# Projections of three gates made ahead and kept in DRAM, in a two-layer trunk kernel

## The chip, the cores and the metric

The kernel runs on one core of one Trainium2 chip. The metric is device time in microseconds: 1871.26 us, median of three runs (1866.83 to 1872.24). The profile below is of one further execution, 1869.99 us.

## The reference

Two layers over 2048 positions of width 1024. Layer 0 mixes with a gated short convolution, layer 1 with gated causal window means. Each mixer is followed by a gate that adds a projection of a 256 wide embedding `p` of the position. This projection, `p[i] @ ple_w_proj[i]`, depends on the inputs only.

```python
h = x
for i in range(DEPTH):                       # DEPTH = 2
    hn = rmsnorm(h, norm_mix[i])
    if i % 2 == 0:
        h = h + short_conv_mixer(hn, a_w_in, a_w_conv, a_w_out)
    else:
        h = h + pool_mixer(hn, b_w_in, b_w_grp, b_scale, b_w_out)
    gate = jax.nn.sigmoid(rmsnorm(h, ple_norm[i]) @ ple_w_gate[i])
    h = h + gate * (p[i] @ ple_w_proj[i])
return rmsnorm(h, final_norm)
```

## The kernel before

Positions lie in four chunks (`ch` 0 to 3) of 512 columns, features in eight tiles of 128 partitions. All products run in a split form: an operand is cast to a high part (ScalarE) and its remainder is taken (VectorE), and `mm` adds three matmuls, high by high (L202), high by low (L203), low by high (L204). So each weight and each activation tile costs one cast on ScalarE and one subtraction on VectorE (L106 and L107 for a loaded block of 128x1024, called a granule; L230, L231 and L236, L237 for an activation tile).

Granules come in the order of a list `order`, with a look-ahead `look` of three (one in the head). The pools are small: 4 raw blocks, 4 split weights, 28 split activations (`act`), 10 tiles `h`, 10 work tiles `wk`, 7 banks of PSUM (`mm`). Granules of kind "w" split into the weight ring, those of kind "p" (embedding) and "pt" (projection and group weights) into `act` tiles. All loads and stores are issued by SyncE's queue, in order.

The stages: a head; then twice (super-chunk `sc`) `mixer_a` for two chunks together, with products in pairs (`pair_steps`) whose 28 operands x11, x21, t2, t1, t3, x22, t4 (four tiles each) are sums of normalised x tiles; then for each of the two chunks `mixer_out` (L573), `gate(0)` (L604), `mixer_b`, `mixer_out` and `gate(1)`.

A gate makes for each of eight tiles `k` 24 matmuls of the dense product and 6 of the projection (`gate_mm`, L584), and `gate_out` (L597) multiplies by the root of the mean square `rb`, takes the sigmoid, multiplies by the projection (L601) and adds to `h` (L602). Until `rb` is there tiles are held in PSUM. The mean square comes from `Stat`: squares on ScalarE, additions on GpSimd (L260), then `fin1` and `fin2`, two small matmuls with ones and a few VectorE steps. `finals` multiplies the finished chunk by its scale, eight operations on VectorE at once (L627), and stores it; `hooks` call such pieces between the products of the next stage.

In the head x of chunks 0 and 1 is loaded, its squares are added by sixteen fp32 matmuls with ones (L717), then normalised (L473), subtracted and added (L476) and split (L231). Beside it `fold` multiplies the group weights of the pooling mixer into its input weights, 48 matmuls of 256 columns for each of four folds, kept in DRAM (`wcomb`). Folds 0 and 1 stand in the head, 2 and 3 (`late_folds`, L735) inside the first pairs.

The operands of the second super-chunk are prepared earlier: `prepare(kk)` (four normalisations L473, four sums L476) writes them to `n_dram`, called at tile 2 of `gate(1)` of chunk 0, of `mixer_out` A, of `gate(0)` and of `mixer_out` B of chunk 1. In `gate(1)` of chunk 1, the turn, `X.ahead` loads and splits two of them per tile, 14 of 28.

The order of instructions on each engine is set when the kernel is built, by a scheduler; on the chip each engine takes its own in that order.

Of the kernel before, what the change touches and what calls it, by code (L numbers as in the profile page):

```python
# [9 lines left out]
F32 = mybir.dt.float32  # L10
# [5 lines left out]
P = 128  # L16
# [30 lines left out]
def trunk_kernel(ctx: ExitStack, tc: tile.TileContext, xT, xN, pT, wts, par, out):  # L47
# [112 lines left out]
    def gate_order(layer, ch):  # L160
        base = W_GATE[layer]
        r = [("p", layer * NCH + ch)]
        for h in range(2):
            r += [("pt", base + 8 + h)] + [("w", base + 4 * h + o) for o in range(4)]
        return r

    for ch in range(NCH):
        if ch % 2 == 0:
            order += [("sum", (0, 0)), ("sum", (1, 0))]
            order += [("pt", W_GRP + 1), ("w", W_UT + 4), ("w", W_UT + 5)] if ch == 0 else []  # L170
            order += [("sum", (0, 1))]
            order += [("w", W_UT + 6), ("w", W_UT + 7)] if ch == 0 else []
            order += [("sum", (0, 2)), ("sum", (0, 3))]
# [37 lines left out]
    def psum():  # L211
        return pm.tile([P, T], F32, tag="mm", name="mm")
# [187 lines left out]

    def mixer_a(sc, X, between):
        ys = []
        for j in range(KT):
            cv_steps, zb_steps = pair_steps(2 * j, X), pair_steps(2 * j + 1, X)
            if j == 0:
                next(cv_steps)
                next(zb_steps)
                between(0)
                next(cv_steps)
                between(1)  # L410
            cs1, cs2, v1, v2 = pair_of(cv_steps)
# [172 lines left out]
    def gate_mm(w, wp, pt, a, k, c0, c1):  # L584
# [19 lines left out]
    def gate(layer, ch, a, hs, s_in, next_gain, extra):  # L604
        hooks.extend([s_in.fin1, s_in.fin2])
        s = Stat()
        nxt = []
        pt = next_granule(("p", layer * NCH + ch))
        base = W_GATE[layer]
        held = []  # L610
        for k in range(KT):
            if k % 4 == 0:
                wp = next_granule(("pt", base + 8 + k // 4))
            held.append((k,) + gate_mm(next_granule(("w", base + k)), wp, pt, a, k, 0, T))
            if s_in.rb is None:
# [106 lines left out]
    load_chunk(0)  # L722
    square_sums(0)
    wg = load_granule(("pt", W_GRP))
    us = [load_granule(("w", W_UT + i)) for i in range(2)]
    fold(0, wg, us)
    load_chunk(1)
    square_sums(1)
    X = Operands(first_operand(x, stats))
    X("x11")  # L730
    us = [load_granule(("w", W_UT + 2 + i)) for i in range(2)]
    fold(1, wg, us)
    wg2 = []

    def late_folds(i):  # L735
        if i == 0:
            wg2.append(next_granule(("pt", W_GRP + 1)))
        fold(2 + i, wg2[0], [next_granule(("w", W_UT + 4 + 2 * i + c)) for c in range(2)])
        if i == 1:
            look[0] = LOOK  # L740

# [102 lines left out]
```

## Time and profile before

| | before |
|---|---|
| median of 3 runs | 1871.26 us (1866.83 to 1872.24) |
| profiled execution | 1869.99 us, span 1868.2 us |
| TensorE (PE) busy | 1819.3 us, 97% |
| VectorE (DVE) busy | 1298.1 us, 69% |
| ScalarE (ACT) busy | 746.4 us, 40% |
| GpSimd (POOL) busy | 261.6 us, 14% |
| mean granted TensorE clock | 0.990 |

Busy shares are means over stages. A window of the trace is read by the count of TensorE's instructions in it, since a waiting or slow TensorE shows as fewer of them. A timeline row gives the start, the length, the line, and in brackets the idle time before the instruction and what ended it.

### The profile page before, as it was taken

How to read it: one execution, taken by the hardware profiler on the slowest of the kernel's cores; microseconds unless marked ns; L12 is line 12 of the kernel's file. 1: busy time of each engine (PE TensorE's matmuls, PEld its weight loads, DVE VectorE, ACT ScalarE, POOL GpSimd, SP SyncE). 2: the span in 40 equal slices, each digit the busy share in tenths (PEclk: the TensorE clock that was granted, in tenths of full speed). 3: DMA queues.
4: the chain of work that ended last, by engine and by line, in shares of the span. 5: the costliest groups of instructions: out<-in, count | busy, mean ns of one | idle time of the engine just before them, and what ended most of it. 6: DMA issues, size and time to landing. Idle time of an engine off the chain costs nothing.

```text
span 1868.2 us, 21507 instructions
## 1 busy us (share of the span) xinstructions
PE 1819.3 (97%) x8217; PEld 1499.2 (80%) x8217; DVE 1298.1 (69%) x1777; ACT 746.4 (40%) x1076; POOL 261.6 (14%) x233
## 2 busy tenths in 40 slices
PE   8799999999999998999998999999999999999997
PEld 5688888888888886888876888888888888888897
DVE  5966766676686766787677665766658666768665
ACT  6533333354345434433443333334433344443332
POOL 1000000021212121211110000001121122120010
PEclk9899999999999999999999999999999999999999
DMA  7311111262343455334534111115323242622221
GB/s 271 113 62 62 68 62 62 85 197 87 109 154 125 176 191 182 121 101 150 170 115 141 53 60 63 65 65 175 124 79 102 91 147 102 203 79 96 97 91 46
DMA packets 70647, 212.21 MB, mean 114 GB/s; under 512 B 7824, under 2 KB 9872, under 8 KB 70544
## 3 DMA queue, kind: packets, MB, share of 16 engines
q1 hardware_dynamic: 70544, 210.84, 33.1%
q8 instruction: 64, 1.05, 0.2%
q14 instruction: 39, 0.32, 0.1%
HBM read 186.69 MB, written 24.12 MB: 113 GB/s over the span
## 4 chain that ended last, share of the span: by engine, by line
PE 92%; DVE 4%; DMA 2%; ACT 1%; issue 1%; SPq 0%; POOL 0%; DVEq 0%; ACTq 0%
PE mm L204 30%; PE mm L202 30%; PE mm L203 30%; DMA out_dram<-h 1%; DMA raw<-in_wts_dram 1%; DVE w L107 1%; DVE h L627 1%; ACT w L106 0%; PE tot L270 0%; PE mm L717 0%; DMA h<-in_xT_dram 0%; DVE act L231 0%; DMA xn<-in_xT_dram 0%; DVE o L667 0%; DVE wk L473 0%
## 5 line engine op out<-in xcount | busy, mean ns | idle before, releaser
L202 PE MATMUL mm<-act,w 128*128 128x512 f32 (+1 forms) x2560 | 972.8, 384 | 22.5 <-ACT act L230 10.3
L203 PE MATMUL mm<-act,w 128*128 128x512 f32 (+1 forms) x2560 | 978.4, 383 | 10.1 <-DVE act L237 5.4
L204 PE MATMUL mm<-act,w 128*128 128x512 f32 (+1 forms) x2560 | 967.6, 383 | 2.1 <-DVE w L107 2.0
L202 PEld LDWEIGHTS mm<-act,w 128*128 128x128 f32 x2560 | 483.1, 189 | 124.0 <-ACT act L230 11.3
L203 PEld LDWEIGHTS mm<-act,w 128*128 128x128 f32 x2560 | 482.9, 189 | 106.7 <-DVE act L231 7.3
L106 ACT CAST w<-raw 128x1024 fp32r<-128x1024 f32 (+1 forms) x296 | 296.1, 1006 | 681.1 <-PE mm L204 456.9
L204 PEld LDWEIGHTS mm<-act,w 128*128 128x128 f32 x2560 | 482.1, 189 | 97.6 <-DVE w L107 4.3
L107 DVE TENSOR_TENSOR w<-raw,w 128x1024 fp32r<-128x1024 f32 (+1 forms) x296 | 345.4, 1170 | 148.0 <-ACT w L106 147.3
L260 POOL TENSOR_TENSOR acc<-acc,wk 128x512 f32<-128x512 f32 x97 | 149.6, 1542 | 552.7 <-ACT wk L257 552.4
L365 DVE TENSOR_TENSOR wk<-mm,wk 128x512 f32<-128x512 f32 x96 | 66.0, 688 | 140.5 <-PE mm L204 140.1
L236 ACT ACTIVATE act<-h,par_sb 128x512 fp32r<-128x512 f32 x96 | 68.9, 719 | 70.0 <-DVE h L602 49.8
L237 DVE SCALAR_TENSOR_TENSOR act<-h,par_sb,act 128x512 fp32r<-128x512 f32 x96 | 88.5, 929 | 8.9 <-ACT act L236 8.7
L578 DVE TENSOR_TENSOR h<-mm,h 128x512 f32<-128x512 f32 x64 | 43.2, 686 | 72.7 <-PE mm L204 61.3
L360 ACT COPY wk<-mm 128x512 f32<-128x512 f32 x96 | 53.0, 582 | 93.1 <-PE mm L204 93.1
L257 ACT ACTIVATE wk<-h 128x512 f32<-128x512 f32 (+1 forms) x119 | 71.0, 597 | 46.0 <-DVE h L602 37.3
L231 DVE TENSOR_TENSOR act<-wk,act 128x512 fp32r<-128x512 f32 x82 | 58.4, 722 | 31.8 <-ACT act L230 31.8
L230 ACT CAST act<-wk 128x512 fp32r<-128x512 f32 x82 | 49.4, 617 | 72.2 <-DVE wk L569 47.8
L415 POOL COPY wk<-uh 128x2 f32<-128x2 f32 x16 | 16.5, 1029 | 364.4 <-DVE wk L365 245.0
L599 DVE TENSOR_TENSOR wk<-mm,rb 128x512 f32<-128x512 f32 (+1 forms) x72 | 44.2, 625 | 29.8 <-PE mm L204 21.4
L107 DVE TENSOR_TENSOR w<-s,w 128x1024 fp32r<-128x1024 f32 x32 | 40.2, 1256 | 31.8 <-ACT w L106 31.6
L552 DVE TENSOR_TENSOR wk<-wk 128x512 f32<-128x512 f32 (+5 forms) x80 | 55.5, 693 | 2.9
L281 POOL TENSOR_TENSOR r<-ms,nhalf 128x8 f32<-128x8 f32 x17 | 28.9, 1700 | 190.3 <-DVE ms L279 190.3
(111 smaller groups left out, 1251.9 us busy)
## 6 DMA issues: line engine op xcount, KB each, us to landing
raw<-in_wts_dram SPq DMA_DIRECT2D x254, 512.0 KB, 3.3
raw<-wcomb SPq DMA_DIRECT2D x32, 512.0 KB, 3.3
h<-in_xT_dram SPq DMA_DIRECT2D x32, 256.0 KB, 5.2
wk<-ndr SPq DMA_DIRECT2D x28, 256.0 KB, 3.8
out_dram<-h SPq DMA_DIRECT2D x24, 256.0 KB, 2.4
wcomb<-wc SPq DMA_DIRECT2D x16, 256.0 KB, 3.0
ydr<-wk SPq DMA_DIRECT2D x16, 256.0 KB, 2.0
raw<-in_pT_dram SPq DMA_DIRECT2D x8, 512.0 KB, 3.2
```

What stands on the lines that cost most here:

```text
L106: nc.scalar.copy(out=hi[:, c], in_=raw[:, c])
L107: eng.tensor_tensor(out=lo[:, c], in0=raw[:, c], in1=hi[:, c].bitcast(F32), op=ALU.subtract)
L202: nc.tensor.matmul(out=ps, lhsT=wh, rhs=ah, start=first, stop=False, skip_group_check=skip)
L203: nc.tensor.matmul(out=ps, lhsT=wh, rhs=al, start=False, stop=False, skip_group_check=skip)
L204: nc.tensor.matmul(out=ps, lhsT=wl, rhs=ah, start=False, stop=last, skip_group_check=skip)
L231: nc.vector.tensor_tensor(out=a[:, 1, :], in0=y, in1=a[:, 0, :].bitcast(F32), op=ALU.subtract)
L236: nc.scalar.activation(out=a[:, 0, :], in_=h, func=AF.Copy, scale=pcol(gcol))
L237: nc.vector.scalar_tensor_tensor(out=a[:, 1, :], in0=h, scalar=pcol(gcol), in1=a[:, 0, :].bitcast(F32), op0=ALU.mult, op1=ALU.subtract)
L257: nc.scalar.activation(out=sq, in_=h, func=AF.Square)
L260: (eng or nc.gpsimd).tensor_tensor(out=acc, in0=acc, in1=sq, op=ALU.add)
L365: nc.vector.tensor_tensor(out=o, in0=ps, in1=c, op=ALU.add)
L552: nc.vector.tensor_tensor(out=nxt[:, lo:end], in0=cur[:, lo:end], in1=cur[:, lo - step:end - step], op=ALU.add)
```

## The change

- `ple(layer, chs)` makes the projections of given gates ahead: 6 matmuls a tile, a copy to a work tile, a store to `p_dram`. Gates (0,0) and (0,1) (layer, chunk) are made in the head, gate (1,1) between `mixer_b` and `mixer_out` B of chunk 1. These gates load each tile from `p_dram` and do 24 matmuls a tile. In the head the two gates share the projection's granules.
- All four folds stand in the head, and the head's granules follow `order`; three of them are loaded ahead of x. `late_folds` goes.
- The squares of the head are added on VectorE (14 additions) and go through `fin1` instead of the sixteen fp32 matmuls.
- `prepare` is called at the last tile of a stage: `gate(1)` of chunk 0, `gate(0)`, `mixer_b` and `mixer_out` B of chunk 1.
- `X.ahead` makes three operands per tile at the turn, two at the last: 23 of 28.

```diff
+PLE_EARLY = ((0, 0), (0, 1), (1, 1))
...
+        if (layer, ch) in PLE_EARLY:
+            return [("w", base + o) for o in range(KT)]
...
+    for g in range(4):
+        order += [("pt", W_GRP + g // 2)] if g % 2 == 0 else []
+        order += [("w", W_UT + 2 * g), ("w", W_UT + 2 * g + 1)]
+    order += ple_order(0, 0, (0,)) + ple_order(0, 1, (1,))
...
-                between(0)
-                next(cv_steps)
-                between(1)
+                look[0] = LOOK
...
+    def ple(layer, chs):
+
+        pts, wps = {}, []
+        base = W_GATE[layer] + 8
+        for h in range(2):
+            if h < len(chs):
+                pts[chs[h]] = next_granule(("p", layer * NCH + chs[h]))
+            wps.append(next_granule(("pt", base + h)))
+        for h in range(2):
+            for ch in chs:
+                pt = pts[ch]
+                for k in range(4 * h, 4 * h + 4):
+                    ps = psum()
+                    for i in range(2):
+                        mm(ps, wps[h], ((k % 4) * 2 + i) * P,
+                           (pt[0][:, i * T:(i + 1) * T], pt[1][:, i * T:(i + 1) * T]), i == 0, i == 1)
+                    e = wtile()[:, :T]
+                    nc.scalar.copy(out=e, in_=ps)
+                    nc.sync.dma_start(out=p_dram[layer, ch][:, k, :], in_=e)
...
+            if early:
+                e = wtile()[:, :T]
+                nc.sync.dma_start(out=e, in_=p_dram[layer, ch][:, k, :])
+                held.append((k, dense(("w", base + k), a), e))
...
-        tot = psum()
-        for i in range(0, KT, 2):
-            sq = acts.tile([P, 2, T], F32, tag="act", name="sq")
-            for k in (i, i + 1):
-                nc.scalar.activation(out=sq[:, k - i, :], in_=x[t][k], func=AF.Square)
-                nc.tensor.matmul(out=tot, lhsT=ones_s, rhs=sq[:, k - i, :], start=k == 0, stop=k == KT - 1)
-        s.root(tot.rearrange("p (a b) -> p a b", b=64))
-        s.fin2()
+        for k in range(KT):
+            s.add(x[t][k], nc.vector)
...
+    prefetch(2)
     load_chunk(0)
     square_sums(0)
...
+    fold_next(0)
     load_chunk(1)
+    roots(0)
+    fold_next(1)
     square_sums(1)
     X = Operands(first_operand(x, stats))
     X("x11")
...
+    fold_next(2)
+    roots(1)
+    X("x21")
+    fold_next(3)
+    X("t2")
+    ple(0, (0, 1))
...
-        return lambda k: prepare(kk, rbs) if k == 2 else None
+        return lambda k: prepare(kk, rbs) if k == KT - 1 else None
...
-            a, s = mixer_out(W_AOUT, ys, hs, 0, preparing(1) if turn else nop)
-            a, s = gate(0, ch, a, hs, s, G_MIX + 8, preparing(2) if turn else nop)
-            ys = mixer_b(ch, a, s, gather if ch == 0 else nop)
+            a, s = mixer_out(W_AOUT, ys, hs, 0)
+            a, s = gate(0, ch, a, hs, s, G_MIX + 8, preparing(1) if turn else nop)
+            ys = mixer_b(ch, a, s, gather if ch == 0 else preparing(2) if turn else nop)
+            if (1, ch) in PLE_EARLY:
+                ple(1, (ch,))
...
-                    X.ahead(2 if k < KT - 1 else 0)
+                    X.ahead(3 if k < KT - 1 else 2)
...
-                if ch == 0 and k == 2:
+                if ch == 0 and k == KT - 1:
                     prepare(0, rbs)
```

The order of instructions shows three places. First TensorE in the head. Before, the last of the 48 pair products with x11 and x21 (512 columns, `act_487` and `act_491` are split tiles of x21) stand ahead of a fold (256 columns, `w_548` and `w_553` its weights):

```order
L203 MATMUL mm_511<-act_487,w_463 128x512
L204 MATMUL mm_511<-act_487,w_463 128x512
L202 MATMUL mm_511<-act_491,w_463 128x512
L203 MATMUL mm_511<-act_491,w_463 128x512
L204 MATMUL mm_511<-act_491,w_463 128x512
L202 MATMUL mm_567<-act_514,w_548 128x256
L203 MATMUL mm_567<-act_515,w_548 128x256
L204 MATMUL mm_567<-act_514,w_548 128x256
L202 MATMUL mm_567<-act_514,w_553 128x256
```

After, fold 3 ends (`w_581`) and the projections of the head follow; `act_586` and `act_587` are the high and low part of chunk 0's embedding, `act_690` and `act_691` of the first projection weights, `act_696` of chunk 1's embedding:

```order
L213 MATMUL mm_650<-act_343,w_581 128x256
L214 MATMUL mm_650<-act_342,w_581 128x256
L212 MATMUL mm_711<-act_586,act_690 128x512
L213 MATMUL mm_711<-act_587,act_690 128x512
L212 MATMUL mm_721<-act_586,act_690 128x512
L213 MATMUL mm_721<-act_587,act_690 128x512
L212 MATMUL mm_731<-act_586,act_690 128x512
L213 MATMUL mm_731<-act_587,act_690 128x512
L212 MATMUL mm_741<-act_586,act_690 128x512
L213 MATMUL mm_741<-act_587,act_690 128x512
L212 MATMUL mm_751<-act_696,act_690 128x512
L212 MATMUL mm_761<-act_696,act_690 128x512
```

And the last projection stands ahead of the first pair product (`act_440` a tile of x11, `w_708` the first pair weights):

```order
L212 MATMUL mm_861<-act_696,act_702 128x512
L213 MATMUL mm_861<-act_697,act_702 128x512
L214 MATMUL mm_861<-act_696,act_703 128x512
L212 MATMUL mm_872<-act_440,w_708 128x512
L213 MATMUL mm_872<-act_440,w_708 128x512
L214 MATMUL mm_872<-act_440,w_708 128x512
```

The pair products with x11 and x21 moved from ahead of the third fold to behind all folds and 96 projections; eleven projection products without the low part of their weights stand first.

Second VectorE in the head, behind the normalisation of chunk 1. Before, the tiles of t2 are split (`act_645` to `act_666`) and pair weights follow:

```order
L476 TENSOR_TENSOR x_173<-x_173,x_171 128x512
L231 TENSOR_TENSOR act_652<-x_167,act_652 128x512
L476 TENSOR_TENSOR x_177<-x_177,x_175 128x512
L231 TENSOR_TENSOR act_659<-x_171,act_659 128x512
L231 TENSOR_TENSOR act_666<-x_175,act_666 128x512
L107 TENSOR_TENSOR w_720<-raw_718,w_720 128x1024
L476 TENSOR_TENSOR x_163<-x_305,x_163 128x512
L107 TENSOR_TENSOR w_725<-raw_556,w_725 128x1024
```

After, the splits of the embedding and the projection's weights (`act_691`, `act_697`, `act_703`) stand behind them:

```order
L241 TENSOR_TENSOR act_671<-x_186,act_671 128x512
L484 TENSOR_TENSOR x_196<-x_196,x_194 128x512
L241 TENSOR_TENSOR act_678<-x_190,act_678 128x512
L241 TENSOR_TENSOR act_685<-x_194,act_685 128x512
L109 TENSOR_TENSOR act_691<-raw_688,act_690 128x1024
L109 TENSOR_TENSOR act_697<-raw_694,act_696 128x1024
L484 TENSOR_TENSOR x_182<-x_298,x_182 128x512
L109 TENSOR_TENSOR act_703<-raw_700,act_702 128x1024
L484 TENSOR_TENSOR x_186<-wk_302,x_186 128x512
L484 TENSOR_TENSOR x_190<-wk_306,x_190 128x512
L109 TENSOR_TENSOR w_876<-raw_874,w_876 128x1024
```

Three granule splits for the projections moved in between t2's splits and the next operands, and one (`act_587`) stands ahead of the normalisation.

Third VectorE in the middle, where `mixer_out` of chunk 1 ends and gate (0,1) begins. Before, `prepare(1)` (`xn`, `tn`) and three splits into `act` (`act_5368`, `act_5406`, `act_5548`) stand among the scalings of the gate's operands (L237):

```order
L107 TENSOR_TENSOR w_5486<-raw_5484,w_5486 128x1024
L473 SCALAR_TENSOR_TENSOR xn_5273<-xn_5273,par_sb_90,rb_4346 128x512 x2
L473 SCALAR_TENSOR_TENSOR xn_5277<-xn_5277,par_sb_90,rb_4353 128x512 x2
L476 TENSOR_TENSOR tn_5284<-xn_5277 128x512
L578 TENSOR_TENSOR h_5122<-mm_5446,h_5122 128x512
L476 TENSOR_TENSOR tn_5283<-tn_5284,xn_5273 128x512
L107 TENSOR_TENSOR w_5491<-raw_5489,w_5491 128x1024
L476 TENSOR_TENSOR tn_5283<-xn_5277,tn_5283 128x512
L476 TENSOR_TENSOR tn_5284<-xn_5273,tn_5283 128x512
L237 SCALAR_TENSOR_TENSOR act_5322<-h_5114,par_sb_90,act_5322 128x512
L237 SCALAR_TENSOR_TENSOR act_5359<-h_5116,par_sb_90,act_5359 128x512
L107 TENSOR_TENSOR act_5368<-raw_5365,act_5367 128x1024
```

After, the same place has only additions to `h` (L586), weight splits and scalings (L247):

```order
L109 TENSOR_TENSOR w_5494<-raw_5492,w_5494 128x1024
L586 TENSOR_TENSOR h_5257<-mm_5366,h_5257 128x512
L109 TENSOR_TENSOR w_5531<-raw_5529,w_5531 128x1024
L586 TENSOR_TENSOR h_5259<-mm_5423,h_5259 128x512
L586 TENSOR_TENSOR h_5261<-mm_5460,h_5261 128x512
L247 SCALAR_TENSOR_TENSOR act_5412<-h_5257,par_sb_90,act_5412 128x512
L247 SCALAR_TENSOR_TENSOR act_5449<-h_5259,par_sb_90,act_5449 128x512
L586 TENSOR_TENSOR h_5263<-mm_5497,h_5263 128x512
L247 SCALAR_TENSOR_TENSOR act_5486<-h_5261,par_sb_90,act_5486 128x512
L109 TENSOR_TENSOR w_5568<-raw_5566,w_5568 128x1024
L586 TENSOR_TENSOR h_5265<-mm_5534,h_5265 128x512
L247 SCALAR_TENSOR_TENSOR act_5523<-h_5263,par_sb_90,act_5523 128x512
```

`prepare(1)` and the three splits left this place; `prepare(0)` moved to just ahead of the eight final scalings that precede these rows.

## Rows read from the trace of the kernel before

**Rows 1.** Busy time per engine and share of the chain that ended last, from the page:
```profile
PE 1819.3 (97%) x8217; PEld 1499.2 (80%) x8217; DVE 1298.1 (69%) x1777; ACT 746.4 (40%) x1076; POOL 261.6 (14%) x233
PE 92%; DVE 4%; DMA 2%; ACT 1%; issue 1%; SPq 0%; POOL 0%; DVEq 0%; ACTq 0%
```

**Rows 2.** Windows: start:end, length, busy (x instructions) per engine, PEclk, DMA share, GB/s:
```profile
365.00:465.00 100.00, 100.00 (x442) 82.75 (x441) 67.39 (x80) 44.31 (x61) 18.44 (x12) 1.00 0.41 135
```

**Rows 3.** Timeline of TensorE in the head (start, length, engine, line, what; idle before):
```profile
61.09 0.79 PE L202 MATMUL mm<-act,w 128*128 128x512 f32 x1 [6.81 <-ACT act L230]
64.78 0.80 PE L203 MATMUL mm<-act,w 128*128 128x512 f32 x1 [2.90 <-DVE act L231]
67.94 0.43 PE L204 MATMUL mm<-act,w 128*128 128x512 f32 x1
90.32 0.50 PE L204 MATMUL mm<-act,w 128*128 128x512 f32 x1 [0.73 <-DVE w L107]
```

**Rows 4.** Windows of the middle:
```profile
700.00:720.00 20.00, 13.50 (x49) 10.41 (x48) 18.28 (x23) 10.29 (x14) 3.36 (x2) 0.83 0.74 260
720.00:740.00 20.00, 19.53 (x86) 15.72 (x85) 7.36 (x11) 4.74 (x6) 1.65 (x1) 1.00 0.30 104
```

**Rows 5.** Windows of the turn:
```profile
960.00:980.00 20.00, 17.74 (x77) 13.98 (x75) 9.85 (x13) 8.67 (x15) 1.67 (x1) 0.98 0.38 132
980.00:1000.00 20.00, 17.15 (x60) 12.49 (x60) 15.60 (x25) 7.73 (x13) 1.84 (x2) 0.85 0.39 132
1000.00:1020.00 20.00, 15.90 (x62) 12.42 (x62) 19.43 (x32) 7.03 (x11) 0.79 (x2) 0.91 0.47 171
1020.00:1040.00 20.00, 19.50 (x85) 15.47 (x85) 11.21 (x15) 6.35 (x9) 0.18 (x1) 1.00 0.16 52
```

**Rows 6.** Window of the head around the first pairs:
```profile
54.50:90.54 36.04, 23.44 (x113) 18.81 (x114) 34.88 (x54) 20.84 (x40) 4.62 (x3) 0.86 0.37 119
```

**Rows 7.** Timeline of VectorE in the head:
```profile
24.01 2.36 DVE L107 TENSOR_TENSOR w<-raw,w 128x1024 fp32r<-128x1024 f32 x2 [2.23 <-ACT w L106]
26.29 5.39 DVE L473 SCALAR_TENSOR_TENSOR x<-x,par_sb,rb 128x512 f32<-128x512 f32 x8
50.99 1.41 DVE L473 SCALAR_TENSOR_TENSOR x<-x,par_sb,rb 128x512 f32<-128x512 f32 x2
72.34 3.09 DVE L231 TENSOR_TENSOR act<-x,act 128x512 fp32r<-128x512 f32 x5
75.35 1.88 DVE L231 TENSOR_TENSOR act<-wk,act 128x512 fp32r<-128x512 f32 x3
```

**Rows 8.** Lines by form, TensorE, the ones-products:
```profile
L717 PE MATMUL mm<-sq,ones_s 128*128 128x512 f32 x32 | 14.8, 604 | 0.2 <-ACT sq L716 0.2
```

**Rows 9.** Timelines of VectorE and TensorE in the middle:
```profile
703.41 3.76 DVE L473 SCALAR_TENSOR_TENSOR xn<-xn,par_sb,rb 128x512 f32<-128x512 f32 x4
712.15 0.80 PE L203 MATMUL mm<-act,w 128*128 128x512 f32 x1 [5.40 <-DVE act L237]
```

**Rows 10.** Timelines of VectorE and TensorE at the turn:
```profile
973.99 1.36 DVE L231 TENSOR_TENSOR act<-wk,act 128x512 fp32r<-128x512 f32 x2 [5.93 <-ACT act L230]
1005.57 5.38 DVE L627 SCALAR_TENSOR_TENSOR h<-h,par_sb,rb 128x512 f32<-128x512 f32 x8
1012.88 0.50 PE L202 MATMUL mm<-act,w 128*128 128x512 f32 x1 [4.10 <-DVE wk L365]
```

**Rows 11.** DMA issues, from the page:
```profile
wk<-ndr SPq DMA_DIRECT2D x28, 256.0 KB, 3.8
ydr<-wk SPq DMA_DIRECT2D x16, 256.0 KB, 2.0
```

**Rows 12.** Lines (L260 from the page, the others by form):
```profile
L260 POOL TENSOR_TENSOR acc<-acc,wk 128x512 f32<-128x512 f32 x97 | 149.6, 1542 | 552.7 <-ACT wk L257 552.4
L602 DVE TENSOR_TENSOR h<-h,wk 128x512 f32<-128x512 f32 x56 | 38.6, 694 | 1.0
L601 DVE TENSOR_TENSOR wk<-mm,wk 128x512 f32<-128x512 f32 x56 | 37.9, 684 | 5.1 <-ACT wk L600 4.5
```

More of the change, by code (lines that the diff above doesn't have):

```diff
@@ L93, in trunk_kernel @@
     n_dram = [dram.tile([P, 7, T], F32, name=f"ndr{kk}", tag=f"ndr{kk}") for kk in range(4)]
+    p_dram = {key: dram.tile([P, KT, T], F32, name=f"pdr{key[0]}{key[1]}", tag=f"pdr{key[0]}{key[1]}") for key in PLE_EARLY}
     y_dram = [dram.tile([P, T], F32, name=f"ydr{j}", tag=f"ydr{j}") for j in range(2 * KT)]
@@ L165, in gate_order, with ple_order @@
         return r
+    def ple_order(layer, ch, halves):
+        return [("p", layer * NCH + ch)] + [("pt", W_GATE[layer] + 8 + h) for h in halves]
+    for g in range(4):
+        order += [("pt", W_GRP + g // 2)] if g % 2 == 0 else []
+        order += [("w", W_UT + 2 * g), ("w", W_UT + 2 * g + 1)]
+    order += ple_order(0, 0, (0,)) + ple_order(0, 1, (1,))
     for ch in range(NCH):
@@ L169, in trunk_kernel @@
             order += [("sum", (0, 0)), ("sum", (1, 0))]
[L170 to L173, printed above, removed]
+            order += [("sum", (0, part)) for part in (1, 2, 3)]
             order += [("sum", (1, part)) for part in (1, 2, 3)]
@@ L179, in trunk_kernel @@
             order += [("comb", j), ("w", W_BZ + j)]
+        if (1, ch) in PLE_EARLY:
+            order += ple_order(1, ch, (0, 1))
         order += [("w", W_BOUT + i) for i in range(8)]
@@ L399, in pair_of, with mixer_a @@
                 return r
-    def mixer_a(sc, X, between):
+    def mixer_a(sc, X):
         ys = []
@@ L607, in gate @@
         nxt = []
-        pt = next_granule(("p", layer * NCH + ch))
+        early = (layer, ch) in PLE_EARLY
+        pt = None if early else next_granule(("p", layer * NCH + ch))
         base = W_GATE[layer]
@@ L611, in gate @@
         for k in range(KT):
-            if k % 4 == 0:
-                wp = next_granule(("pt", base + 8 + k // 4))
-            held.append((k,) + gate_mm(next_granule(("w", base + k)), wp, pt, a, k, 0, T))
+            if early:
+                e = wtile()[:, :T]
+                nc.sync.dma_start(out=e, in_=p_dram[layer, ch][:, k, :])
+                held.append((k, dense(("w", base + k), a), e))
+            else:
+                if k % 4 == 0:
+                    wp = next_granule(("pt", base + 8 + k // 4))
+                held.append((k,) + gate_mm(next_granule(("w", base + k)), wp, pt, a, k, 0, T))
             if s_in.rb is None:
@@ L711, in square_sums, with roots, fold_next @@
         s = Stat()
-        tot = psum()
-        for i in range(0, KT, 2):
-            sq = acts.tile([P, 2, T], F32, tag="act", name="sq")
-            for k in (i, i + 1):
-                nc.scalar.activation(out=sq[:, k - i, :], in_=x[t][k], func=AF.Square)
-                nc.tensor.matmul(out=tot, lhsT=ones_s, rhs=sq[:, k - i, :], start=k == 0, stop=k == KT - 1)
-        s.root(tot.rearrange("p (a b) -> p a b", b=64))
-        s.fin2()
-        stats.append(s)
+        for k in range(KT):
+            s.add(x[t][k], nc.vector)
+        stats.append(s)
+    def roots(t):
+        stats[t].fin1()
+        stats[t].fin2()
+    wg = []
+    def fold_next(g):
+        if g % 2 == 0:
+            wg.append(next_granule(("pt", W_GRP + g // 2)))
+        fold(g, wg[-1], [next_granule(("w", W_UT + 2 * g + c)) for c in range(2)])
+    prefetch(2)
     load_chunk(0)
     square_sums(0)
-    wg = load_granule(("pt", W_GRP))
-    us = [load_granule(("w", W_UT + i)) for i in range(2)]
-    fold(0, wg, us)
+    fold_next(0)
     load_chunk(1)
+    roots(0)
+    fold_next(1)
     square_sums(1)
@@ L730, in trunk_kernel @@
     X("x11")
[L731 to L740, printed above, removed]
+    fold_next(2)
[4 more added lines that the diff above has]
+    ple(0, (0, 1))
     sums_n = const.tile([P, 8], F32, name="sums_n")
@@ L757, in preparing @@
     def preparing(kk):
-        return lambda k: prepare(kk, rbs) if k == 2 else None
+        return lambda k: prepare(kk, rbs) if k == KT - 1 else None
     for sc in range(2):
-        ya = mixer_a(sc, X, nop if sc else late_folds)
+        ya = mixer_a(sc, X)
         ys = [split_act(y) for y in ya]
@@ L767, in trunk_kernel @@
             hs = load_x(ch)
-            a, s = mixer_out(W_AOUT, ys, hs, 0, preparing(1) if turn else nop)
-            a, s = gate(0, ch, a, hs, s, G_MIX + 8, preparing(2) if turn else nop)
-            ys = mixer_b(ch, a, s, gather if ch == 0 else nop)
+            a, s = mixer_out(W_AOUT, ys, hs, 0)
+            a, s = gate(0, ch, a, hs, s, G_MIX + 8, preparing(1) if turn else nop)
+            ys = mixer_b(ch, a, s, gather if ch == 0 else preparing(2) if turn else nop)
+            if (1, ch) in PLE_EARLY:
+                ple(1, (ch,))
             a, s = mixer_out(W_BOUT, ys, hs, 1, preparing(3) if turn else nop)
```

## The prediction

> **What bounds the kernel now.** I read the page's busy times and its chain first. TensorE is busy for 1819.3 of 1868.2 us, and 92% of the chain that ended last is its own work [rows 1]. So the time is TensorE's instructions plus the places where it stands still. Then I read windows for the price of an instruction: in a stretch without waits 442 products of 512 columns go through in 100 us, 0.226 us each, or 90 in 20 us [rows 2]. With 90 as the measure the losses show. Three stretches matter. In the head TensorE has nothing for 6.81 us before its product at 61.09, so from 54.3, gets the next at 64.78, runs at the half clock until 67.94, and waits for weights once more at 90.32 [rows 3]. In the middle (gate 0 of chunk 1 begins) the windows have 49 and 86 products instead of 90, 45 missing, 10.2 us [rows 4]. At the turn to the second half they have 77, 60, 62 and 85, 76 missing, 17.2 us [rows 5]. Elsewhere TensorE is saturated, so work taken from it counts in full there, and work moved between its full stretches counts nothing.
>
> The sum is made against the profiled execution, 1869.99 us (span 1868.2 and 1.8 around it), which is 1.27 below the median of 1871.26. I add that at the end.
>
> **Projections out of two gates.** Gates (0,0) and (0,1) each lose 8 tiles x 6 = 48 products. They stand in stages without waits, so 96 x 0.226 = 21.7 us go. The place of the first gate's weights in the look-ahead is unchanged. In gate (1,1) 48 products go, too, but `ple(1,(1,))` puts the same 48 ahead of that chunk's `mixer_out`, between products: 0.
>
> **The head, the dearest term.** The same 96 products now run in the head, where they cost as much as they push back the first pair. First, where before stands: 113 products fall in 54.5 to 90.5 [rows 6], by the order 48 of a fold and 65 of pairs, and it has 48 pair products ahead of that, so 112 are done when the one at 90.32 begins. At 0.226 us they are worth 25.3 us: the pairs behave as if they had begun at 90.3 - 25.3 = 65.0 and had never waited.
>
> Now after. Its TensorE order is strict: 192 fold products, 96 projections, then the first pair product. The projections need their splits on DVE, which stand behind the operands of the pairs. DVE prices by pitch, from the stretch in [rows 7]: a weight split 1.14 us (two from 24.01 to 26.29), a scaled normalisation 0.67 (eight in 5.39), a plain operation 0.60 (five from 72.34 to 75.35). Three granules now load ahead of x; I put the normalisation of chunk 0 at about 30 instead of 26.29, four later. From there to the normalisation of chunk 1 before spends 24.7 us (26.29 to 50.99). After leaves out the sums of pair 0 (four operations and a split, 3.5 us) and one addition (0.6) there, and adds one act split (1.14); taking 21.6 us, chunk 1 is normalised from 51.6. Then come 8 normalisations (5.4), 12 subtractions and additions (7.2), 4 operand splits (2.4), one weight split and the low half of the first projection weights (2.3), done at 68.9. TensorE's order has 11 projection products ahead that need only what ScalarE casts and an earlier split; they fill the wait, and the 12th stands for 68.9. The 14 additions that replace the ones-products lie, I estimate, in DVE's idle time before 24 us and between x0's splits.
>
> From 68.9 the other 85 take 19.2 us. TensorE will have idled since about 50, as it did from 54, and before's restart ran at the half clock to 67.94: eight products at 0.43 instead of 0.226, 1.6 us. The first pair product starts at 89.7, 24.7 later than the virtual 65.0. Operands and weights are ready by then (DVE's own queue up to its first addition ends near 91, and that addition waits for products anyway), so nothing is late behind it. The 32 records of the ones-products, 14.8 us [rows 8], leave TensorE but paid nothing, since folds waited for DVE and loads anyway. All four folds lie in the time in which TensorE waits. Head against gates: +24.7 - 21.7 = +3.0. Bounds: if chunk 1's normalisation comes at 48, 3.6 less; if at 55, 3.4 more; if the projections begin when before's first product did, at 61 to 62, about 7 less.
>
> **The middle, 10.2 us.** `prepare(1)` stands there on DVE: four normalisations 3.76 us and four operations of 0.60, 6.2 us, and three act splits of 1.14 [rows 9]; TensorE waits 5.40 for an operand scaled behind them. Both leave: the preparation goes to the end of the gate, the splits to the head. What is late next is the finals' burst: `prepare(0)` now lies just ahead of it, and 68 instead of 59 products stand between the sum and the broadcast that releases it, 2.0 us later, and h's buffers come free with it. I take -7 of 10.2; ends -2 (the burst makes the same gap) and -9.
>
> **The turn, 17.2 us.** Before makes 14 of 28 operands ahead. DVE waits 5.93 us there for casts whose loads came late, and a burst of eight final scalings, 5.38 us, holds the addition for which TensorE waits 4.10 [rows 10]. 43 of the 76 missing products lie before 1000 us (9.7 us), 33 behind it (7.5 us). With 23 made, 5 loads, casts and splits are left, so I take 9 of 9.7. The burst stays, so I take 1 of 7.5. That is -10; ends -5 and -14. Its cover is narrow: in the shorter gate a tile gives DVE 24 x 0.226 = 5.4 us, and asks three products and sums of `gate_out` at 0.60 (1.8), a weight split (1.14) and three operand splits (1.8), 4.7 us.
>
> **Edits at nothing.** `prepare(2)` and (3) lie beside full TensorE stages before and after. The 24 loads of made projections and 24 stores are transfers off TensorE; a load of the same size took 3.8 us to land, a store 2.0 [rows 11]. If a load comes late, gate_out holds one bank of PSUM where it held two; that cover gone, a gate waits some us. Two granules fewer are loaded.
>
> The load adds one wait: the multiplication by the projection (`gate_out`, third line) waits for SP's transfer, and on DVE the next tile's weight split is queued behind it, for which TensorE waits in turn. A tile is 5.4 us and a load 3.8, and DVE reaches that multiplication only when the tile's own products are done: I take nothing, and 1 us for each load that is a full tile late, at most 24.
>
> **Sum.** 1869.99 - 21.7 + 24.7 - 7 - 10 = 1856.0; with the 1.27 to the median 1857.3, so 1857.
>
> **Rivals.**
> B, the head overlaps: DVE reaches the first projection split at 62, so the pairs start at 62 + 19.2 + 1.6 = 82.8, +17.8; both stalls go nearly whole (-9, -14): 1843.1 + 1.3 = 1844. For it: before had its first product at 61.09. Against: six act splits instead of two stand in one DVE queue that was busy for 34.9 of 36.0 us there [rows 6].
> C, the stalls move: the finals' burst holds the middle (-2), the operands wait for their loads again (-5): 1866.0 + 1.3 = 1867. For it: the burst is untouched, and 4.7 of 5.4 us is tight. Against: 6.2 + 3.4 us of DVE really leave the middle.
> D, slower, by the projections' stores: the 16 results leave TensorE by 7 banks and work tiles, of which 6 of 10 hold x of chunk 1, so 4 are free. SP issues in order, and the stores are behind raw loads that wait for DVE splits. If the stores don't move before DVE is through at 91, TensorE stops at tile 12: 66 products less the 11 ahead, 12.4 us after 70.5, at 82.9. It waits 8 us and restarts at the half clock, some 2: +10. With no gain at the turn (the operands' loads and the made projections share the same tiles and SP) and -2 in the middle: 1869.99 - 21.7 + 34.7 - 2 = 1881.0 + 1.3 = 1882. It decides once more than 11 tiles wait; one store freed per 1.4 us (a tile's six products) defuses it.
> E, DVE stands still for GpSimd: in the early gates the multiplication by the projection reads two tiles of SBUF instead of PSUM and SBUF, while GpSimd adds squares. If each of gate (1,1)'s 8 waits for one such addition, 1.54 us [rows 12], the tile asks 6.2 us of its 5.4, and 8 x 0.8 = 6 us come back at the turn: 1863. Against: before has the addition with two SBUF inputs beside the same GpSimd work, and it takes 694 ns against 684 for the form with PSUM [rows 12]; 24 x 10 ns = 0.2 us, beside the path. The Trainium skill (SBUF — State Buffer, section "SBUF: two separate sides") has the rule behind this: a DVE operation with two SBUF inputs and a GpSimd operation that reads SBUF share a port pair as an exclusive lock, and the later one blocks for the whole instruction. By that rule the time would be E's, by the rows the forecast's; the trace bears it out for 10 ns only.
>
> **Chances.** A (forecast, 1848 to 1865) 0.47, B 0.15, C (1865 to 1877) 0.18, D 0.17, E 0.03. A measurement of this kernel can't tell 0.3%, 5.6 us: faster is below 1865.6, slower above 1876.9. Faster: A and B, 0.62; within: C and E's worse half with a few late loads, 0.21; slower: D, 0.17. Range 1842 to 1878: it leaves out the worse part of D and the better half of B, 2 in 10.
>
> **What will show it.** In the changed profile: 96 products fewer in the gates and both stages still full at 90 in 20 us; the first pair product near 90 (B: 83; D: a wait of TensorE inside the projections for ScalarE's copy or a bank); the projections' first wait on DVE's act split; the windows of the middle back above 80; those of the turn above 75, with the wait on the first operands gone and the one behind the final scalings still there. The forecast is wrong if the pairs begin before 84 or after 96, or if the middle's or the turn's loss is not smaller than before.

## The result and the profile after

The changed kernel takes 1880.50 us (four runs, 1879.67 to 1882.73) against 1870.84 of before: ratio 1.0057, 95% interval 1.0039 to 1.0075. It is slower by 0.57%; the forecast of 1857 was on the wrong side, and the time lies above its range of 1842 to 1878. The profiled execution has a span of 1878.9 us, 10.7 more.

The page of the changed kernel, for [rows 1]:

```profile
PE 1815.6 (97%) x8189; PEld 1503.2 (80%) x8189; DVE 1304.8 (69%) x1791; ACT 755.2 (40%) x1100; POOL 253.5 (13%) x233
PE 91%; DVE 3%; DMA 2%; ACT 2%; issue 1%; SPq 0%; POOL 0%; DVEq 0%; ACTq 0%
```

TensorE's busy time fell by 3.7 us and the span grew by 10.7: standing still, not work. To find where, I fix three places by one event each: the first of the two small matmuls that sum the squares at the start of a gate. First the kernel before, then the changed one, at gate (0,0), at gate (1,1) of chunk 1 and at gate (0) of chunk 2:

```profile
423.92 0.40 PE L270 MATMUL tot<-acc_hi,ones_r 128*128 128x512 f32 x1
...
908.30 0.40 PE L270 MATMUL tot<-acc_hi,ones_r 128*128 128x512 f32 x1
...
1329.89 0.40 PE L270 MATMUL tot<-acc_hi,ones_r 128*128 128x512 f32 x1
```

```profile
452.56 0.39 PE L280 MATMUL tot<-acc_hi,ones_r 128*128 128x512 f32 x1
...
915.99 0.39 PE L280 MATMUL tot<-acc_hi,ones_r 128*128 128x512 f32 x1
...
1340.62 0.39 PE L280 MATMUL tot<-acc_hi,ones_r 128*128 128x512 f32 x1
```

At the first the changed kernel is 28.6 us late, and has 96 products (21.7 us) behind it that before still has ahead: the head costs 6.9 net. At the second it is 7.7 late with 48 more products done (10.9): it is 3.2 us ahead, so 10.1 us were won between. At the third it is 10.7 late with equal work left: from gate (1,1) to there it lost 13.9 us. 6.9 - 10.1 + 13.9 = 10.7. These are single executions: in the seven profiled kernels whose head is this one the first event lies between 450.42 and 454.48, so a term of the head carries some 2 us either way.

The middle, for [rows 4], is full, and the gate of chunk 0 too:

```profile
460.00:480.00 20.00, 20.00 (x90) 16.54 (x89) 16.66 (x21) 12.48 (x18) 3.22 (x3) 1.00 0.37 124
700.00:720.00 20.00, 20.00 (x90) 16.54 (x89) 16.07 (x21) 8.62 (x12) 4.80 (x4) 1.00 0.82 276
720.00:740.00 20.00, 20.00 (x90) 16.49 (x89) 13.34 (x18) 7.21 (x9) 5.03 (x3) 1.00 0.41 142
```

The turn, for [rows 5]:

```profile
960.00:980.00 20.00, 11.35 (x35) 7.66 (x34) 14.72 (x21) 9.46 (x16) 3.83 (x3) 0.83 0.68 236
980.00:1000.00 20.00, 14.15 (x51) 10.72 (x52) 10.37 (x17) 7.73 (x13) 1.46 (x2) 0.83 0.27 93
1000.00:1020.00 20.00, 18.60 (x73) 14.33 (x73) 17.65 (x28) 7.80 (x13) 1.85 (x2) 0.91 0.23 83
1020.00:1040.00 20.00, 17.31 (x66) 14.10 (x67) 12.65 (x19) 4.18 (x6) 0.58 (x1) 0.83 0.32 115
1040.00:1060.00 20.00, 19.47 (x85) 15.48 (x84) 13.43 (x18) 7.40 (x10) 0.18 (x1) 1.00 0.16 54
```

The counts of TensorE are 35, 51, 73, 66 and 85: 140 of 450 products are missing, 31.7 us, where before missed 76 (its last window, 1040 to 1060, has 90). Its waits there, for [rows 10]:

```profile
967.03 0.79 PE L212 MATMUL mm<-act,w 128*128 128x512 f32 x1 [4.56 <-ACT act L240]
983.16 0.80 PE L212 MATMUL mm<-act,w 128*128 128x512 f32 x1 [6.90 <-ACT wk L370]
...
1022.69 0.79 PE L212 MATMUL mm<-act,w 128*128 128x512 f32 x1 [4.08 <-DVE wk L375]
```

It waits for a cast operand, then for a copy that frees a bank of PSUM, then behind the final scalings as before.

The head, TensorE, for [rows 3]: one long wait, then half speed (0.43 us from product to product) to 72.06, and the first pair product at 92.12.

```profile
68.48 0.79 PE L212 MATMUL mm<-act 128*128 128x512 f32 x1 [15.34 <-ACT act L108]
...
71.21 0.63 PE L212 MATMUL mm<-act 128*128 128x512 f32 x1
71.63 0.63 PE L213 MATMUL mm<-act 128*128 128x512 f32 x1
72.06 0.93 PE L212 MATMUL mm<-act 128*128 128x512 f32 x3
...
92.12 0.39 PE L212 MATMUL mm<-act,w 128*128 128x512 f32 x1
```

VectorE in the head, for [rows 7], normalises chunk 0 from 32.00 and chunk 1 from 54.28:

```profile
32.00 5.39 DVE L481 SCALAR_TENSOR_TENSOR x<-x,par_sb,rb 128x512 f32<-128x512 f32 x8
...
54.28 1.41 DVE L481 SCALAR_TENSOR_TENSOR x<-x,par_sb,rb 128x512 f32<-128x512 f32 x2 [1.19 <-ACT rb L303]
...
70.80 2.35 DVE L109 TENSOR_TENSOR act<-raw,act 128x1024 fp32r<-128x1024 f32 x2
```

ScalarE in the head, its queue in order:

```profile
64.36 1.05 ACT L108 CAST w<-raw 128x1024 fp32r<-128x1024 f32 x1 [9.83 <-DMA raw<-in_wts_dram]
65.31 2.17 ACT L240 CAST act<-x 128x512 fp32r<-128x512 f32 x4
67.39 2.93 ACT L108 CAST act<-raw 128x1024 fp32r<-128x1024 f32 x3
```

A cast of pair weights waits 9.83 us for its load, and the three casts that the projections need stand behind it. SyncE issued that load at 61.15, the first of four:

```profile
61.15 12.36 SPq L102 DMA_DIRECT2D raw<-in_wts_dram  x4
```

### The profile page after: what moved, and what is told of

The parts are those of the page before. It is cut to its first block, busy times and chain, and to the rows that moved or that the text cites. A ratio compares the mean times of both kernels' runs of the same rounds, so it can differ in the third digit from the quotient of the medians.

```text
span 1878.9 us, 21641 instructions
## 1 busy us (share of the span) xinstructions
PE 1815.6 (97%) x8189; PEld 1503.2 (80%) x8189; DVE 1304.8 (69%) x1791; ACT 755.2 (40%) x1100; POOL 253.5 (13%) x233
## 4 chain that ended last, share of the span: by engine, by line
PE 91%; DVE 3%; DMA 2%; ACT 2%; issue 1%; SPq 0%; POOL 0%; DVEq 0%; ACTq 0%
PE mm L212 30%; PE mm L214 30%; PE mm L213 30%; DVE w L109 1%; DMA wk<-ndr 1%; DMA raw<-in_wts_dram 1%; ACT w L108 1%; DVE act L241 0%; PE tot L280 0%; ACT wc L359 0%; DMA wcomb<-wc 0%; ACT wk L267 0%; DVE h L661 0%; DMA wk<-in_xT_dram 0%; DVE wk L629 0%
## 5 line engine op out<-in xcount | busy, mean ns | idle before, releaser
L586 DVE TENSOR_TENSOR h<-mm,h 128x512 f32<-128x512 f32 x64 | 43.4, 688 | 80.1 <-PE mm L214 77.0
L247 DVE SCALAR_TENSOR_TENSOR act<-h,par_sb,act 128x512 fp32r<-128x512 f32 x96 | 92.5, 973 | 7.6 <-ACT act L246 7.5
L212 PE MATMUL mm<-act 128*128 128x512 f32 (+1 forms) x144 | 53.5, 374 | 15.3 <-ACT act L108 15.3
```

Source lines behind the costliest of these rows:

```text
L212: nc.tensor.matmul(out=ps, lhsT=wh, rhs=ah, start=first, stop=False, skip_group_check=skip)
L247: nc.vector.scalar_tensor_tensor(out=a[:, 1, :], in0=h, scalar=pcol(gcol), in1=a[:, 0, :].bitcast(F32), op0=ALU.mult, op1=ALU.subtract)
```

## The experiments

The letters of this section are those of the expectations, not of the prediction's rivals. Theory L: at the turn nine more operands and the made projections turn through the same ten work tiles and one queue of SyncE. Rival E: the loads of made projections are enough. Rival C: the gate is shorter on TensorE, and the side work has lost its cover, that is, the TensorE work behind which it was hidden. "Turn" below is the time from the squares' sum of gate (1,1) to that of gate (0) of chunk 2, read as above; its products alone take 401.4 us (1776) with own projections in the gate, 390.5 (1728) without; what is left over is the loss. The medians of the edited kernels are of 4 to 11 runs, turn and loss of one profiled execution. Each ratio is against the runs of before on the same chip.

| run | median us | ratio (95%) | turn us | loss us |
|---|---|---|---|---|
| before | 1870.84 | 1 | 421.6 | 20.2 |
| changed | 1880.50 | 1.0057 (1.0039 to 1.0075) | 424.6 | 34.1 |
| t1_ahead14 | 1880.84 | 1.0056 (1.0044 to 1.0069) | 425.4 | 34.9 |
| t2_own_proj | 1857.05 | 0.9928 (0.9916 to 0.9941) | 412.2 | 10.8 |
| t3_both_back | 1867.53 | 0.9983 (0.9974 to 0.9992) | 422.6 | 21.2 |
| t4_e_elsewhere | 1877.25 | 1.0036 (1.0023 to 1.0048) | 421.2 | 30.7 |
| u1_cover_back | 1877.14 | 1.0038 (1.0026 to 1.0050) | 418.9 | 17.5 |
| u2_no_loads | 1874.44 | 1.0021 (1.0011 to 1.0030) | 417.6 | 27.1 |
| n1_ple_sooner | 1848.45 | 0.9877 (0.9860 to 0.9893) | 415.3 | 13.9 |
| n2_no_head_proj | 1856.42 | 0.9919 (0.9905 to 0.9934) | 412.6 | 11.2 |
| m1_moves_only | 1862.30 | 0.9949 (0.9935 to 0.9963) | 421.4 | 20.0 |
| b1_moves_ahead23 | 1852.58 | 0.9897 (0.9884 to 0.9911) | 411.6 | 10.2 |
| n3_squares_pool | 1850.39 | 0.9884 (0.9867 to 0.9901) | 415.2 | 13.8 |

**t1_ahead14**, on the changed kernel:
```diff
-                    X.ahead(3 if k < KT - 1 else 2)
+                    X.ahead(2 if k < KT - 1 else 0)
```


> The changed kernel with X.ahead back at 2 operands a tile (0 at the last), 14 of 28; gate (1,1) still loads made projections. At the turn (960 to 1060 us) the changed kernel misses 140 products of 512 columns, 31.7 us, the kernel before 76, 17.2 us. Theory L (nine more operands and the made projections turn through the same ten work tiles and one in-order queue, so the gate ends in lockstep): the loss falls to about that of before, time about 1866 us (1863 to 1870). Rival E (the loads of made projections hold the gate by themselves): no gain, 1878 to 1882. Rival C (the gate is 10.9 us shorter on TensorE, so the same side work has less cover): half the gain, 1870 to 1877.

No gain, 1880.84, as rival E had it: theory L falls. Fewer operands ahead only change which one is waited for:

```profile
974.62 1.22 PE L212 MATMUL mm<-act,w 128*128 128x512 f32 x2 [11.18 <-ACT act L240]
```

**t2_own_proj**:
```diff
-PLE_EARLY = ((0, 0), (0, 1), (1, 1))
+PLE_EARLY = ((0, 0), (0, 1))
```


> The changed kernel with gate (1,1) making its own projections again (out of the list of early gates), X.ahead stays at 3 operands a tile, 23 of 28. Theory L: three operand tiles a k still turn through ten work tiles, with 5 instead of 6 tiles asked per k and 10.9 us more of TensorE work in the gate: part of the loss goes, 1870 to 1877 us. Rival E: the made projections' loads were the cause, so the loss falls below that of before (23 operands made), 1860 to 1866. Rival C: the cover is back, 1863 to 1869.

1857.05, better than any theory said: making gate (1,1)'s projections ahead costs 23.5 us. The windows from 960 and 980 have 83 and 74 products where the changed kernel had 35 and 51 (t2 reaches that gate 11.8 us sooner, so they do not hold quite the same work; the turn column does):

```profile
960.00:980.00 20.00, 18.87 (x83) 15.28 (x82) 12.88 (x19) 10.15 (x17) 2.52 (x3) 1.00 0.27 91
980.00:1000.00 20.00, 17.81 (x74) 12.84 (x72) 18.32 (x30) 8.31 (x13) 3.84 (x3) 1.00 0.57 210
```

**t3_both_back** has both edits.

> The changed kernel with both edits of the turn undone: 14 operands ahead and gate (1,1) with its own projections. All theories: the turn loses what it lost before, 17 us, and what is left of the change is the head (+7.0) and the middle (-10.2): 1865 to 1869 us. If it is above 1873, the head's part or another stage costs more than the alignment of the two traces shows.

As expected, 1867.53. Against t2 nine operands are worth 10.4 us of turn in the long gate; t1 against the changed kernel shows them worth 0.8 in the short one. Of the 10.4, 7.5 are won up to the 327th TensorE instruction behind the squares' sum (82.8 us after it in t3, 75.3 in t2), where the waits for the first operands lie. Most of the rest is that the wait behind the final scalings all but goes; t3, then t2:

```profile
1011.36 0.79 PE L212 MATMUL mm<-act,w 128*128 128x512 f32 x1 [4.10 <-DVE wk L375]
```

```profile
999.94 0.50 PE L212 MATMUL mm<-act,w 128*128 128x512 f32 x1 [0.81 <-DVE wk L375]
```

**t4_e_elsewhere**:
```diff
-                e = wtile()[:, :T]
+                e = hp.tile([P, T], F32, tag="h", name="e") if layer else wtile()[:, :T]
```


> The changed kernel, only that the loaded projection tiles of gate (1,1) lie in the two spare tiles of pool h instead of the ten work tiles; loads, order of the program and 23 operands stay. Theory L with the work tiles as the short resource: 5 instead of 6 per k, the loss of 31.7 us falls by 4 to 10, 1871 to 1877 us. If SP's order alone holds it (the operands' loads behind weight loads that wait for raw buffers), no change, 1878 to 1882. Rival E: the loads themselves are what is waited for and now start earlier, 1866 to 1872.

1877.25, and 3.4 us of the turn: work tiles have a part, a small one.

**u1_cover_back**: gate (1,1) takes its granules and makes its projections beside the loads; only the loaded ones are read.
```diff
...
+                    held.append((k, gate_mm(next_granule(("w", base + k)), wp, pt, a, k, 0, T)[0], e))
...
```


> The changed kernel, but gate (1,1) also makes its 48 projection products and nobody reads them: it still loads and uses the made ones. TensorE has 48 products (10.9 us) more than the changed kernel; loads, work tiles and operands are the changed kernel's. Theory C (the shorter gate lacks cover for DVE's, ScalarE's and SP's side work): the 10.9 us are filled time, the turn loses about 7 us as in t2 instead of 31.7, time 1880.5 - 24 + 10.9 = 1867 us. Rival E (loads of made projections, waiting for a work tile ahead of weights and operands in SP's queue, stretch the gate): the loss stays, 1880 to 1891 us.

**u2_no_loads** reads a tile that is there anyway in place of the loaded ones, so its result lacks this gate's projection:
```diff
-                e = wtile()[:, :T]
-                nc.sync.dma_start(out=e, in_=p_dram[layer, ch][:, k, :])
+                e = wtile()[:, :T] if layer == 0 else s_in.acc
+                if layer == 0:
+                    nc.sync.dma_start(out=e, in_=p_dram[layer, ch][:, k, :])
```


> The changed kernel without the 8 loads of made projections in gate (1,1): an SBUF tile that is there anyway (the squares' sum) stands in their place, so the gate's values leave the projection out; ple(1,(1,)), its stores, 23 operands and the short gate stay. Rival E: the turn's loss falls to that of t2, 1857 to 1860 us. Theory C: the gate is still 10.9 us short, 1872 to 1880. Between, 1862 to 1870, both have a part.

u1, 1877.14, fell between the theories; u2, 1874.44, inside C's range. Both causes have a part. Cover, by the loss column: changed 34.1 to u1 17.5 is 16.6 us; u2 27.1 to t2 10.8 is 16.3. Loads: u1 17.5 to t2 10.8 is 6.7; changed 34.1 to u2 27.1 is 7.0. The medians, with the 10.9 us of u1's extra products taken off, put it at 14.2 and 17.4 for the cover, 9.2 and 6.1 for the loads. So C carries the larger part, 14 to 17 us, and E 6 to 9. u2 frees the work tiles as well, so t4's 3 us belong to the latter. With u1 TensorE does 48 products more than the changed kernel in the turn and finishes it 5.7 us sooner:

```profile
960.00:980.00 20.00, 19.44 (x86) 15.77 (x84) 18.18 (x26) 10.79 (x18) 4.71 (x3) 1.00 0.66 229
980.00:1000.00 20.00, 15.26 (x62) 11.44 (x63) 12.12 (x19) 9.62 (x16) 1.47 (x2) 1.00 0.28 101
```

**n1_ple_sooner**, on t2:
```diff
-    X("t2")
     ple(0, (0, 1))
+    X("t2")
```


> t2 (1857.05 us) with the head's projections called ahead of the t2 operands instead of behind them. On DVE their weight splits move 10 operations forward, to just behind the first subtraction of chunk 1. Theory (the head's price is the wait of TensorE from 53 to 68.5 us for splits that stand late in DVE's order): the projections start at 62 to 66, 1852 to 1854.5. Rival (ScalarE's casts wait for granules whose raw buffers come free late, so DVE's order is not what is waited for): 1856 to 1858.

1848.45, 8.6 less than t2 and below the range expected. The call moves two queues at once: on ScalarE the casts of the projections' granules now precede that of the pair weights, and on VectorE the first split of their weights stands at 60.06 where the changed kernel had it at 70.80. TensorE starts the projections at 56.79, in t2 at 67.87; t2, then two rows of n1:

```profile
67.87 0.80 PE L212 MATMUL mm<-act 128*128 128x512 f32 x1 [15.96 <-ACT act L108]
```

```profile
56.79 0.77 PE L212 MATMUL mm<-act 128*128 128x512 f32 x1 [3.79 <-ACT act L108]
...
60.06 1.22 DVE L109 TENSOR_TENSOR act<-raw,act 128x1024 fp32r<-128x1024 f32 x1
```

Its first pair product stands at 82.60, in t2 at 91.17. At the first event it is 11.1 us ahead of t2, and the turn gives 3.1 back, since the wait behind the final scalings is there again, 3.19 us. What each queue's part is was not separated. It is the fastest version run, 1.2% under before.

**n2_no_head_proj**, on t2:
```diff
-PLE_EARLY = ((0, 0), (0, 1))
+PLE_EARLY = ()
...
-    order += ple_order(0, 0, (0,)) + ple_order(0, 1, (1,))
...
-    ple(0, (0, 1))
```


> t2 (1857.05 us) without projections made ahead: all gates make their own; four folds in the head, moved preparation and 23 operands stay. Theory: the head as changed without the projections starts the pairs some 3 us later than before (normalisation of chunk 1 at 54.3 instead of 51.0), while with them it costs 7.0: 1857 - 4 = 1853 us (1851 to 1855). Rival (the projections are what the head loses, the rest is free): 1850. Rival (they are hidden, the folds and granule order cost the 7): 1857 or more.

1856.42, within 1 us of t2, nearest the third reading. Its squares' sum of gate (0,0) is at 430.24 against 423.92 before, with equal work: the changed head without projections already costs some 6 us (6.3 here), and the projections in it cost what the gates give back, to within 1 us.

**m1_moves_only**, on before:
```diff
-        return lambda k: prepare(kk, rbs) if k == 2 else None
+        return lambda k: prepare(kk, rbs) if k == KT - 1 else None
```
and, as in the change, two of the calls one stage later and `prepare(0)` at the last tile.

> The kernel before with only the four calls of prepare moved to the last tile of a stage (gate (1) of chunk 0, gate (0), mixer_b and mixer_out B of chunk 1). Theory: the middle's loss of 10.2 us goes whole, as in the changed kernel, and nothing else moves: 1870.5 - 10 = 1860 us (1858 to 1862). Rival (the three act splits that also left the middle hold it by themselves, 3.4 us): 1863 to 1866.

Ratio 0.9949, 9.6 us; its windows of the middle have 90 and 90. So moving the preparation is enough, and the three act splits did not hold the middle by themselves:

```profile
700.00:720.00 20.00, 20.00 (x90) 16.49 (x89) 19.07 (x23) 10.39 (x14) 5.94 (x4) 1.00 0.67 214
720.00:740.00 20.00, 20.00 (x90) 16.52 (x89) 14.07 (x20) 10.72 (x16) 2.66 (x3) 1.00 0.22 74
```

**b1_moves_ahead23** adds the diff of `X.ahead` of the change.

> m1 and X.ahead at 3 operands a tile (23 of 28); the head and all gates as before. Theory: the nine operands pay 10 us while the gate makes its own projections, as t2 against t3: 1850 us (1848 to 1852). Then the changed head, without projections (n2, 1856.4), costs some 6 us against the head of before, and the projections in it nearly nothing more. If b1 is at 1856, the head of n2 costs nothing and the turn pays less here.

Ratio 0.9897, 19.3 us. The nine operands pay 9.8 us of turn here too.

**n3_squares_pool**, on n1:
```diff
-            s.add(x[t][k], nc.vector)
+            s.add(x[t][k], nc.vector if t == 0 else nc.gpsimd)
```


> n1 (1848.45 us) with chunk 1's seven square additions in the head on GpSimd instead of DVE. They stand among the steps of chunk 0's root on DVE (22.6 to 30.3 us) and the normalisation of chunk 0 starts at 32.0 instead of 26.3 before. Theory (DVE's queue sets the head): the normalisation comes 3 to 4 us sooner, and the pairs with it, 1844.5 to 1847. Rival (granules and their buffers set the rest of the head): 1847.5 to 1849. Other side (GpSimd's slower additions, 1.5 us each, make chunk 1's root late): 1850 to 1853.

0.9884 against 0.9877: no gain. Chunk 0's normalisation still began at 32.01 and its eight operations now spread over 7.41 us instead of 5.39. The trace shows what does it: the two operations that begin while GpSimd's additions run take 3.44 us together, the six behind them 0.67 us each. GpSimd, then VectorE twice:

```profile
26.69 8.20 POOL L270 TENSOR_TENSOR acc<-acc,wk 128x512 f32<-128x512 f32 x5
32.01 3.44 DVE L481 SCALAR_TENSOR_TENSOR x<-x,par_sb,rb 128x512 f32<-128x512 f32 x2
35.37 4.05 DVE L481 SCALAR_TENSOR_TENSOR x<-x,par_sb,rb 128x512 f32<-128x512 f32 x6
```

## Why the prediction was wrong, step by step

- **Projections out of two gates, 21.7 us**: right. The gate of chunk 0 is full without them, and the difference at the first event is the head's alone.
- **The head, +24.7**: measured 28.6. Chunk 1's normalisation began at 54.28, not 51.6, mostly since chunk 0's began at 32.0, not 30. Behind it VectorE's queue took what I had counted, some 17.7 us to the end of the first projection split at about 72.0, where I had 17.3. So the 2.7 us account for the first pair product, 92.12 against 89.7. The statement that 11 projection products "fill the wait" failed as well: I counted VectorE's queue and not ScalarE's, where the casts stood behind a load of another granule. But it cost nothing that the rows show, since the 12th product needs VectorE's split, and that was done later than these casts; the eight products at the half clock were in the sum. Behind the first pair product 1.5 us more went, 0.9 of them in three waits for weights of 0.4 to 0.5 us where before has one. n2 shows the price is that of the rebuilt head, not of the projections, which I had not thought apart; why the rebuilt head is some 6 us dearer without them was not taken further.
- **The middle, -7**: the mechanism was right, the size 10.1 (m1 alone 9.6). Of the two things that were to leave, the preparation alone is enough. The burst of final scalings, 2 us later, held nothing.
- **The turn, -10**: here the forecast failed. The turn cost 13.9 us instead of giving 10, and that is 23.9 of the 24.7 us between the forecast's -14.0 and the +10.7 of the spans. The nine operands did pay 10, in t3 to t2 (10.4) and m1 to b1 (9.8), but only in a gate that makes its own projections, and that the total fits is in part luck: the wait on operands gave 7.5 where I took 9, the wait behind the final scalings 2 to 3 where I took 1. The step that failed is the one in front, "In gate (1,1) 48 products go, too, but `ple(1,(1,))` puts the same 48 ahead of that chunk's `mixer_out`, between products: 0." The products are neutral in number and not in place: they were TensorE's work in the very stretch in which VectorE, ScalarE and SyncE drain the gate's tiles. Without them the drain ends last, and with the loads of the next point it cost 23 us in place of 0; u1 and u2 put the cover at 14 to 17 of these. I gave the drain 4.7 of 5.4 us a tile and left out of it the sums and splits of the pair weights that the look-ahead puts there; the first steps of three tiles in a row stand 11.0 and 6.0 us apart, and in the longer step VectorE also stood still some 3 us for casts:

```profile
945.85 0.68 DVE L627 TENSOR_TENSOR wk<-mm,rb 128x512 f32<-128x512 f32 x1
...
956.82 0.68 DVE L627 TENSOR_TENSOR wk<-mm,rb 128x512 f32<-128x512 f32 x1
...
962.84 0.68 DVE L627 TENSOR_TENSOR wk<-mm,rb 128x512 f32<-128x512 f32 x1
```

How the drain's end holds TensorE, the gate's last addition on VectorE shows. ScalarE's square stands behind it, and behind that the copy for which TensorE waits 6.90 us until 983.16:

```profile
981.24 0.68 DVE L630 TENSOR_TENSOR h<-h,wk 128x512 f32<-128x512 f32 x1
982.01 0.63 ACT L267 ACTIVATE wk<-h 128x512 f32<-128x512 f32 x1 [2.39 <-DVE h L630]
982.54 1.05 ACT L370 COPY wk<-mm 128x512 f32<-128x512 f32 x2
```

- **"The 24 loads of made projections and 24 stores are transfers off TensorE"**, at nothing: the loads cost 6 to 9 us in gate (1,1) (u1 to t2, u2 to the changed kernel), none in the two gates that had no operands to make beside them.
- **Rivals.** D gave 1882, near the measured time, by luck: its +10 in the head did not come, TensorE did not wait once inside the projections, and the window from 80 to 100 has 90 products. Its middle of -2 measured -10.1. Its "no gain at the turn" was the nearest of all rivals, but it is 13.9 us short and names tiles and SyncE's queue, the smaller cause. B did not come. C's "operands wait for their loads again" is seen in part, in a turn 19 us dearer than C allowed. E's price is not there: the multiplication with two SBUF inputs takes as long as that with PSUM:

```profile
L629 DVE TENSOR_TENSOR wk<-mm,wk 128x512 f32<-128x512 f32 x32 | 21.7, 685 | 2.5 <-ACT wk L628 2.1
L629 DVE TENSOR_TENSOR wk<-wk 128x512 f32<-128x512 f32 x24 | 16.1, 683 | 3.3 <-DMA wk<-pdr 3.0 <-ACT wk L628 0.3
```

But in the trace none of these 24 multiplications overlaps an operation of GpSimd, so they do not test E's rule, and neither does the prediction's mean of 694 ns over all additions. Where two such operations meet, VectorE does stand still. In gate (0,0) of the changed kernel the scaling of an operand (L247), which reads two tiles of SBUF, takes 0.75 us, and 1.61 when it begins inside GpSimd's addition:

```profile
475.14 1.29 POOL L270 TENSOR_TENSOR acc<-acc,wk 128x512 f32<-128x512 f32 x1 [3.30 <-ACT wk L267]
475.37 1.61 DVE L247 SCALAR_TENSOR_TENSOR act<-h,par_sb,act 128x512 fp32r<-128x512 f32 x1
...
483.87 0.75 DVE L247 SCALAR_TENSOR_TENSOR act<-h,par_sb,act 128x512 fp32r<-128x512 f32 x1 [0.19 <-ACT act L246]
```

By the Trainium skill (SBUF — State Buffer, "SBUF: two separate sides") such an operation of VectorE and one of GpSimd that reads SBUF lock each other out for a whole instruction. The trace agrees with it here and in n3.


## What to carry to other kernels

Work of the bounding engine that is moved out of a stage, even at equal count, shortens the stage's cover: before booking it at nothing, add up all that the other engines do in that stage, granules of the next one included, against the time that is left. Here 10.9 us moved cost 14 to 17. And a wait in the head is read on every in-order queue between a load and its user: the projections' casts stood behind another load's cast on ScalarE and their splits behind the next operands on VectorE, and calling one function a line sooner, which moved both, gave 8.6 us.

## What the runs showed that I had not expected

The costs of cover and of the loads are of one size whichever is taken away first (14 to 17 and 6 to 9 us), as far as a spread of some 3 us between profiled executions and medians lets one say, while the nine operands are worth 10 us with the cover and nothing without it. And the longer waits of the changed kernel were followed by a stretch at the half clock: after the 15.34 us in the head the products came 0.43 us apart for 3.6 us, and so they did for a while after the waits of 4.56, 6.90 and 4.08 us at the turn. In the window of t1 with the 11.18 us wait the mean granted clock was 0.74.

```profile
960.00:980.00 20.00, 8.82 (x31) 6.59 (x30) 12.41 (x19) 10.05 (x17) 4.82 (x4) 0.74 0.49 170
```
